# A decoder trunk on one core: every engine's order from a recorded plan instead of hand-set delays and a scheduler

## The chip, the cores and the metric

The kernel runs on one core of a Trainium2 chip. A core has four compute engines with a queue each: TensorE (PE in the profile; PEld is its loading of stationary operands), VectorE (DVE), ScalarE (ACT) and GpSimd (POOL). SyncE (SP) issues most DMAs, and ACT and POOL issue some. The metric is the time of one execution in device microseconds (us), lower is better. Before the change three runs took 1003.58, 1005.42 and 1005.6 us, a median of 1005.42 us.

## The reference, cut to what matters

A trunk of two layers over 256 tokens of width 1024, all in float32. Each layer is a SwiGLU FFN at half weight, a token mixer beside four memory cross-attention heads with one output projection, and a second FFN. Layer 0 mixes with an mLSTM (four heads), layer 1 with windowed attention (sixteen query heads, two key heads, a learned sink per head).

```
mem_kv = rms_norm(mem, mem_norm_g) @ mem_w_kv
for i in range(2):
    x = x + 0.5 * swiglu(rms_norm(x, ffn1_norm_g[i]), ffn1_w_in[i], ffn1_w_out[i])
    hn = rms_norm(x, mix_norm_g[i])
    proj = hn @ (a_w_in if i == 0 else b_w_in)
    y_tok = mlstm_heads(proj...) if i == 0 else swa_heads(proj...)
    y_mem = memory_heads(proj[..., -512:], mem_k, mem_v, ...)
    x = x + concatenate([y_tok, y_mem]) @ w_out
    x = x + 0.5 * swiglu(rms_norm(x, ffn2_norm_g[i]), ffn2_w_in[i], ffn2_w_out[i])
```

## The kernel before, in words

**Products.** Activations are held transposed, 128 features by 256 tokens a tile. Each float32 product with a weight is made of three products of rounded operands (`mm3`, L226): the high half of one side and of the other, and the two cross terms. So every weight tile of 128 x 1024 that a DMA brings (`wr`, five buffers, issued by SP at L220) is split: ACT casts it to its rounded half `wh` (L213) and DVE subtracts to get the rest, `wl` (L214). `wh` and `wl` have eight buffers each. A tile feeds 24 matmuls. In most stages the weight is the stationary operand; in the memory projection and in some groups of both mixers (`rows=True`) the activation is stationary and the weight moves.

**Stages.** `memory()` warms TensorE with 18 matmuls (L432), projects the memory and spawns the chains that finish its keys and the first norm. Then come FFN 1, mixer A, FFN 2, FFN 1 of layer 1, mixer B and the last FFN. In an FFN, `ffn_in` runs eleven groups of two PSUM banks, and `hidden` (L513) turns each into a unit. `out_proj` (L657) takes four banks at its first row of weights and waits, row by row, for the heads it multiplies.

**Chains.** Everything that isn't a weight product (norms, attention heads, transposes) is a Python generator, a chain, that yields an estimated delay in microseconds between its steps. `Weave` (L61) holds a clock `now`, which each matmul call advances by a fixed amount, and after every yield of the main program it runs the chain steps whose delay has passed. The delays are in `LAT` (L53). So the order of TensorE's queue is the order in which `Weave` calls things. In mixer B a head (L952) has three steps on TensorE: scores of two banks (L962, L967), six transposes (L995), and the product with the values (L1004).

**Who orders what.** `manual_schedule` (L1031) is given for PE and SP alone: these two issue in program order. DVE, ACT and POOL are ordered by the framework's scheduler, from its own model of durations. Three places bind it: a table load is issued after the last activation that needs the old table (L140), the copies of raw memory keys after the last weight cast (L455), the splits of x0 too (L490). All engines run their queues in order. PSUM has eight banks (`pb8`), one pool of 31 units (`up`) holds most intermediate tiles.

**Late constants.** `late_constants` (L184) is a chain called in the first FFN, at group 5. It has five small DMAs on POOL's queue and one of 192 KB (the mask), and small DVE operations on what they bring, among them `nsink` (L196).

Of the kernel before, what the change touches and what calls it, by code (L numbers as in the profile page):

```python
# [2 lines left out]

# [6 lines left out]

F32 = mybir.dt.float32
F32R = mybir.dt.float32r
# [48 lines left out]
class Weave:  # L61
# [4 lines left out]


    def __init__(self):
        self.now, self.live, self.seq = 0.0, [], 0

    def spawn(self, chain, delay=0.0):
        self.live.append([self.now + delay, self.seq, chain])
# [1 line left out]

    def step(self, c):
        self.now = max(self.now, c[0])
        try:
            c[0] = self.now + next(c[2])
        except StopIteration:
            self.live.remove(c)  # L80

    def ready(self):
        c = [c for c in self.live if c[0] <= self.now]
# [11 lines left out]
            self.step(min(self.live, key=lambda c: (c[0], c[1])))  # L95


@with_exitstack
def tile_trunk(ctx: ExitStack, tc: tile.TileContext, a, out):
    nc = tc.nc  # L100
    seq = [0]

    def mk(pool, shape, dt, tag):
        seq[0] += 1
        return pool.tile(shape, dt, tag=tag, name=f"{tag}_{seq[0]}")

    def pool(name, bufs, **kw):
        return ctx.enter_context(tc.tile_pool(name=name, bufs=bufs, **kw))

    cst = pool("cst", 1)  # L110
    onesr = mk(cst, [P, P], F32R, "onesr")
    nc.vector.memset(onesr.bitcast(F32), 1.0 / D)
    wv = Weave()


    xhp = pool("xhp", 4)
# [11 lines left out]
    pb8 = pool("pb8", 8, space=PSUM)  # L128

    tt = nc.vector.tensor_tensor  # L130
    tabled = [None]

    def act(*args, **kw):
        ins = nc.scalar.activation(*args, **kw)  # L134
        if args[2] not in (AF.Copy, AF.Square):
            tabled[0] = ins
# [66 lines left out]


    pieces = [1]
    last = [None]

    def split(src, shape):
        hi = mk(whp, shape, F32R, "wh")
        lo = mk(wlp, shape, F32R, "wl")  # L210
        n = shape[1] // pieces[0]
        for i in range(pieces[0]):
            last[0] = nc.scalar.copy(hi[:, i * n:(i + 1) * n], src[:, i * n:(i + 1) * n])  # L213
            tt(out=lo[:, i * n:(i + 1) * n], in0=src[:, i * n:(i + 1) * n],  # L214
               in1=hi[:, i * n:(i + 1) * n].bitcast(F32), op=ALU.subtract)
        return hi, lo
# [209 lines left out]
    def memory():  # L426

        idle = tmp().rearrange("p a b -> p (a b)")[:, :T].bitcast(BF16)
        nc.vector.memset(idle, 0.0)
        bank = mo()  # L430
        for i in range(WARM):
            nc.tensor.matmul(bank, idle[:, :P], idle, start=True, stop=True, skip_group_check=True)  # L432
# [72 lines left out]
        wv.spawn(sums(), LAT['x0'])  # L505
        wv.spawn(finish(raw), LAT['finish'])
# [513 lines left out]
    def program():  # L1020
        yield from memory()
        x1, x2, x3 = Norm(G_MIX, half=False, cols=True), Norm(G_F2), Norm(G_F1 + 8)
        x4, x5 = Norm(G_MIX + 8, rows=False), Norm(G_F2 + 8)
        yield from ffn(x0, a["ffn1_w_in"][0], a["ffn1_w_out"][0], x1, late_constants)
        yield from mixer_a(x1, x2)
        yield from ffn(x2, a["ffn2_w_in"][0], a["ffn2_w_out"][0], x3)
        yield from ffn(x3, a["ffn1_w_in"][1], a["ffn1_w_out"][1], x4, rope_tables)
        yield from mixer_b(x4, x5)
        yield from ffn(x5, a["ffn2_w_in"][1], a["ffn2_w_out"][1])

    with tc.manual_schedule(engines={mybir.EngineType.PE, mybir.EngineType.SP}):  # L1031
        wv.run(program())


def by_chunk(rows):
# [35 lines left out]
```

## Time and profile before

| | |
|---|---|
| median of three runs | 1005.42 us |
| the profiled execution, by its own time | 1004.76 us |
| its span, first to last instruction | 1003.0 us |
| granted TensorE clock | 1.00 |
| HBM read, over the span | 180.32 MB, 181 GB/s |
| PE instructions | 8560 matmuls, as many weight loads |
| DVE, ACT, POOL instructions | 1080, 779, 27 |

The span begins with the first instruction on any engine and leaves out 1.76 us of the execution's time. A line of the timeline has a start, a duration, engine, source line and tiles, and in brackets the idle time of that engine just before, with what ended it. Matmuls overlap: one of 256 columns is shown as 0.28 us long, while the next starts 0.11 us later, so starts are compared with starts. The line of an activation is often L134 and that of a weight product L227, L228 or L229, since a helper issues them; the tiles tell which is meant.

### The profile page before, as it was taken

What the parts mean: (1) busy time and instruction counts of PE and PEld (TensorE: products, weight loads), DVE (VectorE), ACT (ScalarE), POOL (GpSimd) and SP (SyncE); (2) the same over time, 40 slices, a digit from 0 to 9 for tenths busy, and PEclk for the clock granted to TensorE, in tenths of its full rate; (3) what the DMA queues carried; (4) which work ended last, traced back from release to release, by engine and by line L of the source; (5) the groups of instructions that cost most, each with busy time, mean ns of one, the idle gap of its engine ahead of it and who ended that gap; (6) DMA issues with size and microseconds to landing.
All of it is one profiled execution on the core that took longest, in us unless ns stands there. A gap on an engine that the chain in (4) does not pass through costs nothing.

```text
span 1003.0 us, 20581 instructions
## 1 busy us (share of the span) xinstructions
PE 993.9 (99%) x8560; PEld 975.7 (97%) x8560; DVE 664.6 (66%) x1080; ACT 531.9 (53%) x779; POOL 29.4 (3%) x27
## 2 busy tenths in 40 slices
PE   8999999999999999999999999999999999999998
PEld 6999999999999999999999999999997899999998
DVE  5897665578756686666568666656777767666551
ACT  5765445456666554444445444545577755544440
POOL 1001000000101000000000000000122000000000
PEclk9999999999999999999999999999999999999999
DMA  9777655666634566665666666566641247666550
GB/s 308 256 225 214 192 181 179 199 179 193 188 129 145 169 210 190 193 198 177 190 204 201 197 196 191 171 198 200 195 142 64 89 146 228 193 195 188 184 168 22
DMA packets 173204, 182.70 MB, mean 182 GB/s; under 512 B 7124, under 2 KB 168328, under 8 KB 173112
## 3 DMA queue, kind: packets, MB, share of 16 engines
q1 hardware_dynamic: 171872, 179.60, 57.8%
q8 instruction: 67, 1.10, 0.4%
q10 hardware_dynamic: 1016, 1.58, 0.4%
q0 software_dynamic: 224, 0.22, 0.2%
q14 instruction: 25, 0.20, 0.1%
HBM read 180.32 MB, written 1.05 MB: 181 GB/s over the span
## 4 chain that ended last, share of the span: by engine, by line
PE 93%; ACT 3%; DVE 2%; DMA 1%; issue 0%; SPq 0%; ACTq 0%; DVEq 0%
PE bank L227 30%; PE bank L229 30%; PE bank L228 30%; PE bank L233 2%; ACT u L134 1%; PE bank L238 1%; ACT wh L213 1%; DMA wr<-in_mem_w_kv_dram 1%; DVE wl L214 1%; PE bank L1004 1%; ACT xh L134 0%; DVE col L972 0%; DVE acc L282 0%; PE bank L304 0%; DVE col L971 0%
## 5 line engine op out<-in xcount | busy, mean ns | idle before, releaser
L214 DVE TENSOR_TENSOR wl<-wr,wh 128x1024 fp32r<-128x1024 f32 (+1 forms) x347 | 414.5, 1197 | 268.4 <-ACT wh L213 267.1
L213 ACT CAST wh<-wr 128x1024 fp32r<-128x1024 f32 (+1 forms) x347 | 356.9, 1031 | 385.8 <-PE bank L228 357.6
L227 PE MATMUL bank<-xh,wh 128*128 128x256 f32 x1544 | 428.0, 277 | 0.0
L229 PE MATMUL bank<-xh,wl 128*128 128x256 f32 x1544 | 426.8, 276 | 0.1
L228 PE MATMUL bank<-xl,wh 128*128 128x256 f32 x1544 | 426.7, 276 | 0.0
L229 PEld LDWEIGHTS bank<-xh,wl 128*128 128x128 f32 x1544 | 290.1, 188 | 0.3 <-DVE wl L214 0.3
L227 PEld LDWEIGHTS bank<-xh,wh 128*128 128x128 f32 x1544 | 290.0, 188 | 0.1
L228 PEld LDWEIGHTS bank<-xl,wh 128*128 128x128 f32 x1544 | 289.9, 188 | 0.1
L227 PE MATMUL bank<-u,wh 128*128 128x256 f32 x896 | 249.3, 278 | 0.0
L228 PE MATMUL bank<-u,wh 128*128 128x256 f32 x896 | 247.6, 276 | 0.0
L229 PE MATMUL bank<-u,wl 128*128 128x256 f32 x896 | 247.6, 276 | 0.0
L227 PEld LDWEIGHTS bank<-u,wh 128*128 128x128 f32 x896 | 168.3, 188 | 1.7 <-issue 1.7
L228 PEld LDWEIGHTS bank<-u,wh 128*128 128x128 f32 x896 | 168.3, 188 | 0.1
L229 PEld LDWEIGHTS bank<-u,wl 128*128 128x128 f32 x896 | 168.2, 188 | 0.0
L227 PE MATMUL bank<-wh,xh 128*128 128x256 f32 x208 | 59.6, 287 | 0.5 <-ACT t L997 0.5
L228 PE MATMUL bank<-wl,xh 128*128 128x256 f32 x208 | 57.9, 278 | 0.0
L229 PE MATMUL bank<-wh,xl 128*128 128x256 f32 x208 | 57.8, 278 | 0.0
L516 DVE TENSOR_TENSOR t<-bank,rb 128x256 f32<-128x256 f32 x88 | 36.1, 420 | 6.8 <-PE bank L229 6.8
L227 PEld LDWEIGHTS bank<-wh,xh 128*128 128x128 f32 x208 | 39.1, 188 | 1.2 <-ACT t L997 0.7
L228 PEld LDWEIGHTS bank<-wl,xh 128*128 128x128 f32 x208 | 39.1, 188 | 0.1
L229 PEld LDWEIGHTS bank<-wh,xl 128*128 128x128 f32 x208 | 39.0, 188 | 0.0
L134 ACT ACTIVATE u<-bank,col,col 128x256 f32<-128x256 f32 (+1 forms) x48 | 24.9, 530 | 15.2 <-DVE col L975 7.9
(183 smaller groups left out, 674.1 us busy)
## 6 DMA issues: line engine op xcount, KB each, us to landing
wr<-in_ffn_w_in_dram SPq DMA_DIRECT2D x176, 512.0 KB, 4.5
wr<-in_ffn_w_out_dram SPq DMA_DIRECT2D x80, 512.0 KB, 3.8
wr<-in_a_w_in_dram SPq DMA_DIRECT2D x28, 512.0 KB, 3.8
wr<-in_b_w_in_dram SPq DMA_DIRECT2D x14, 512.0 KB, 4.3
wr<-in_a_w_out_dram SPq DMA_DIRECT2D x12, 512.0 KB, 3.2
wr<-in_b_w_out_dram SPq DMA_DIRECT2D x12, 512.0 KB, 3.2
wr<-in_ffn_w_out_dram SPq DMA_DIRECT2D x16, 256.0 KB, 2.8
wr<-in_mem_w_kv_dram SPq DMA_DIRECT2D x7, 512.0 KB, 8.1
```

The source lines that it names most:

```text
L134: ins = nc.scalar.activation(*args, **kw)
L213: last[0] = nc.scalar.copy(hi[:, i * n:(i + 1) * n], src[:, i * n:(i + 1) * n])
L214: tt(out=lo[:, i * n:(i + 1) * n], in0=src[:, i * n:(i + 1) * n], in1=hi[:, i * n:(i + 1) * n].bitcast(F32), op=ALU.subtract)
L227: nc.tensor.matmul(ps, wh, xh, start=start, stop=False, skip_group_check=True)
L228: nc.tensor.matmul(ps, wh, xl, start=False, stop=False, skip_group_check=True)
L229: nc.tensor.matmul(ps, wl, xh, start=False, stop=stop, skip_group_check=True)
L233: nc.tensor.matmul(ps, lhsT, rhs, start=start, stop=stop, skip_group_check=True)
L238: nc.tensor.transpose(ps, src, ident[:k, :k])
L516: tt(out=t[:, m], in0=ps[m][:, :T], in1=x.rb, op=ALU.mult)
L1004: nc.tensor.matmul(o[es[e], cs], vr[:, i, js], pTs[e][:, src], start=i == 0, stop=i == 1, skip_group_check=True)
```

## The change

The program isn't issued while it is written. `tile_trunk` is run against a `Rehearsal`, whose engines only note each operation with the tiles that it reads and writes. `Weave` still gives the order in which operations are noted, and marks the chain step that each belongs to (`current`). From what each operation touches, `note` works out what it must follow. Then `plan` steps through all operations with a formula for each duration and returns one order, and `perform` issues the operations in it. `manual_schedule` now holds for all engines, so ACT, DVE and POOL too run in the planned order.

In `plan`, SP's DMAs keep their order. TensorE's work is cut into runs: an operation of the main program is a run of its own and these keep their order; a chain step is one run, and any of the first 24 not yet issued may go when its inputs are ready. A single chain run that is ready beside a ready main run is held back until a second one is ready, or for at most `HOLD` = 3 us. A main matmul that opens a new PSUM bank is passed over while `SPARE` = 2 or fewer banks are free and chain runs remain. On ACT, DVE and POOL the operation goes next that is ready and has the earliest `late` (the latest start that TensorE's order allows); none is planned more than `AHEAD` = 26 us before the matmul that follows it in the noted order. The three bindings of L140, L455 and L490 go; `note` keeps the order of table loads against the activations that need them. Tiles get their buffers in the order of issue. No instruction of the kernel is added or taken away.

```diff
@@ Weave.step
+        self.steps += 1
+        self.current = self.steps
         try:
             c[0] = self.now + next(c[2])
         ...
+        self.current = 0
@@ Rehearsal
+    def perform(self, order):
+        ...
+        for n in order:
+            op = self.ops[n]
+            getattr(getattr(nc, op.engine), op.kind)(*map(real, op.args), ...)
+    def note(self, engine, kind, args, kw):
+        ...
+        for write, vs in ((False, ins), (True, outs)):
+            for v in vs:
+                (a, b), (p0, p1) = v.extent(), v.parts
+                for o, c, d, q0, q1, w in v.tile.uses:
+                    same = o.engine == engine == "tensor"
+                    if (write or w) and (same or a <= d and c <= b and q0 < p1 and p0 < q1):
+                        behind(o, "data")
+        ...
+        if engine == "scalar":
+            if kind == "preload_act_table_set":
+                for o in self.tabled:
+                    behind(o, "order")
+                self.table, self.tabled = op, []
+            elif kind == "activation" and args[2] not in (AF.Copy, AF.Square):
+                if self.table is not None:
+                    behind(self.table, "order")
+                self.tabled.append(op)
@@ constants and durations
+AHEAD = 26.0
+SPARE = 2
+SWITCH = 0.1
+HOLD = 3.0
+OVERLAP = 0.085
+LATENCY = dict(tensor=0.25, vector=0.08, scalar=0.08, gpsimd=0.12, dma=0.0)
+def duration(op):
+    ...
+    if "dma" in kind:
+        return 0.06 if e != "gpsimd" else 0.6
+    if e == "tensor":
+        ...
+        if mv.dt == F32R:
+            return 0.1135 if st.tile.key[0] in ("wlp", "whp", "cst") else 0.117
+        if mv.dt == BF16 or st.dt == BF16:
+            return moving / 2400
+        half = st.shape[0] == 64 or st.shape[1] == 64
+        return moving * (0.00169 if not half else 0.00085)
+    if e == "vector":
+        ...
+        return 0.15 + 0.001045 * n + (0.09 if kind == "tensor_tensor_reduce" else 0)
+    if e == "scalar":
+        ...
+        t = 0.207 + 0.000825 * op.outs[0].size
+        ...
+    return 0.2 + 0.29 * n
@@ plan
+        if now:
+            found.append((free["tensor"], now[0], None))
+        else:
+            t0 = free["tensor"]
+            head = main[at["main"]] if at["main"] < len(main) else None
+            r0 = ready(head[0]) if head else None
+            if head and tiles_of[head[0].n] and side and len(places[tiles_of[head[0].n][0].key]) <= SPARE:
+                r0 = None
+            best, there = None, 0
+            for run in side[:24]:
+                r = run_ready(run)
+                if r is not None:
+                    there += r <= t0
+                    if best is None or max(r, t0) < best[0]:
+                        best = (max(r, t0), run, r)
+            if best and last_kind and there < 2 and t0 - best[2] < HOLD and r0 is not None and r0 <= t0:
+                best = None
+            if best and (r0 is None or best[0] <= max(r0, t0)):
+                found.append((best[0], best[1][0], best[1]))
+            elif r0 is not None:
+                found.append((max(r0, t0), head[0], head))
+        ...
+        for e in loose:
+            cand = []
+            for k, (n, op) in enumerate(loose[e].items()):
+                ...
+                r = ready(op)
+                if r is not None:
+                    cand.append((max(r, due[n] - AHEAD), op))
+            ...
+            t0 = max(free[e], min(c[0] for c in cand))
+            r, op = min((c for c in cand if c[0] <= t0), key=lambda c: (late[c[1].n], c[1].n))
+            ...
+            found.append((max(r, t0), op, None))
@@ tile_trunk and below
-        with tc.issue_after(tabled[0].ins):
-            nc.scalar.preload_act_table_set(name)
+        nc.scalar.preload_act_table_set(name)
-            with tc.issue_after(last[0].ins):
-                nc.scalar.copy(raw, gr.ps)
+            nc.scalar.copy(raw, gr.ps)
-                with tc.issue_after(last[0].ins):
-                    for c2 in range(4):
-                        x0.put(xT[c2], False)
+                for c2 in range(4):
+                    x0.put(xT[c2], False)
-    with tc.manual_schedule(engines={mybir.EngineType.PE, mybir.EngineType.SP}):
-        wv.run(program())
+    wv.run(program())
-    with tile.TileContext(nc) as tc:
-        tile_trunk(tc, aps, out)
+    with tile.TileContext(nc) as tc, ExitStack() as pools:
+        rec = Rehearsal(tc, aps["gd"])
+        tile_trunk(pools, rec, aps, out)
+        with tc.manual_schedule():
+            rec.perform(plan(rec))
```

More of the change, by code (lines that the diff above doesn't have):

```diff
@@ L1 @@
+import bisect
 import math
@@ L8 @@
 from concourse import mybir
-from concourse._compat import with_exitstack
 F32 = mybir.dt.float32
@@ L68, in __init__ @@
     def __init__(self):
-        self.now, self.live, self.seq = 0.0, [], 0
+        self.now, self.live, self.seq, self.current, self.steps = 0.0, [], 0, 0, 0
     def spawn(self, chain, delay=0.0):
@@ new lines, with __init__, real @@
+class Slot:
+    def __init__(self, pool, tag, number, shape, dt, name):
+        self.key, self.pool, self.number, self.uses, self.made = (pool.name, tag), pool, number, [], None
+        self.args = (shape, dt, tag, name)
+    def real(self):
+        if self.made is None:
+            shape, dt, tag, name = self.args
+            self.made = self.pool.real.tile(shape, dt, tag=tag, name=name)
+        return self.made
+class Op:
+    def __init__(self, engine, kind, outs, ins, args, kw):
+        self.engine, self.kind, self.outs, self.ins, self.args, self.kw = engine, kind, outs, ins, args, kw
+        self.after, self.before = {}, []
@@ new lines @@
+AHEAD = 26.0
[5 more added lines that the diff above has]
+def duration(op):
+    kind, e = op.kind, op.engine
+    n = max([v.size for v in op.outs + op.ins] or [0])
+    if "dma" in kind:
+        return 0.06 if e != "gpsimd" else 0.6
+    if e == "tensor":
+        moving = op.outs[0].size
+        if kind == "transpose":
+            return 0.109 if moving > 4 else 0.075
+        st, mv = op.args[1], op.args[2]
+        if mv.dt == F32R:
[5 more added lines that the diff above has]
+    if e == "vector":
+        if kind == "memset":
+            n = op.outs[0].size
+        if kind == "tensor_scalar" and op.ins[0].tile.key[1] != "bank" and n >= 128:
+            return 0.215 + 0.00052 * n
+        return 0.15 + 0.001045 * n + (0.09 if kind == "tensor_tensor_reduce" else 0)
+    if e == "scalar":
+        if kind == "preload_act_table_set":
+            return 1.283
+        t = 0.207 + 0.000825 * op.outs[0].size
+        views = sum(isinstance(op.kw.get(k), View) for k in ("scale", "bias"))
+        return t + 0.08 * views + (0.1 if "accum_out" in op.kw else 0)
+    return 0.2 + 0.29 * n
@@ L101, in tile_trunk @@
+def tile_trunk(ctx: ExitStack, nc, a, out):
     seq = [0]
@@ L107, in pool @@
     def pool(name, bufs, **kw):
-        return ctx.enter_context(tc.tile_pool(name=name, bufs=bufs, **kw))
+        return nc.pool(ctx, name, bufs, **kw)
     cst = pool("cst", 1)
+    wv = nc.weave = Weave()
     onesr = mk(cst, [P, P], F32R, "onesr")
     nc.vector.memset(onesr.bitcast(F32), 1.0 / D)
-    wv = Weave()
     xhp = pool("xhp", 4)
@@ L130, in tile_trunk @@
     tt = nc.vector.tensor_tensor
[L131 to L136, printed above, removed]
+    act = nc.scalar.activation
     def table(name):
-        with tc.issue_after(tabled[0].ins):
-            nc.scalar.preload_act_table_set(name)
+        nc.scalar.preload_act_table_set(name)
     def unit(dt):
@@ L205, in tile_trunk @@
     pieces = [1]
-    last = [None]
     def split(src, shape):
@@ L212, in split @@
         for i in range(pieces[0]):
-            last[0] = nc.scalar.copy(hi[:, i * n:(i + 1) * n], src[:, i * n:(i + 1) * n])
+            nc.scalar.copy(hi[:, i * n:(i + 1) * n], src[:, i * n:(i + 1) * n])
             tt(out=lo[:, i * n:(i + 1) * n], in0=src[:, i * n:(i + 1) * n],
```

278 lines of the change are left out of this document (275 added, 3 removed).

## The prediction

> **What bounds the kernel now.** The first page shows which engine fills the span.
>
> ```profile
> span 1003.0 us, 20581 instructions
> ...
> PE 993.9 (99%) x8560; PEld 975.7 (97%) x8560; DVE 664.6 (66%) x1080; ACT 531.9 (53%) x779; POOL 29.4 (3%) x27
> ...
> PE 93%; ACT 3%; DVE 2%; DMA 1%; issue 0%; SPq 0%; ACTq 0%; DVEq 0%
> ```
>
> TensorE is busy for 99% of the span and holds 93% of the chain that ended last. The change takes no instruction away, so it can only remove time in which TensorE stands still. Two views size that: what TensorE waited for, and its busy time by stage.
>
> ```profile
> engine line waited for: us in total, times, longest us
> PE bank L967 <- ACT u L134: 1.4, 1, 1.4
> PE bank L432 <- DVE t L429: 1.4, 1, 1.4
> PE bank L228 <- DVE wl L214: 0.9, 1, 0.9
> PE bank L227 <- ACT t L997: 0.5, 1, 0.5
> PE bank L227 <- ACT wh L213: 0.4, 1, 0.4
> PE bank L962 <- ACT t L997: 0.2, 1, 0.2
> ```
>
> Those are all of TensorE's waits over 0.15 us, 4.8 us together. The second is the wait for the first memset at the very start, which stays. The third and fifth belong to the first weight tiles. The other three, 2.1 us, are in mixer B.
>
> ```profile
> core 0: us, PE busy (x) PEld busy (x) DVE busy (x) ACT busy (x) POOL busy (x), PEclk, DMA share, GB/s
> 330.00:715.00 385.00, 385.00 (x3399) 385.00 (x3398) 252.28 (x333) 192.21 (x234) 0.00 (x0) 1.00 0.63 193
> 735.00:765.00 30.00, 27.99 (x209) 23.86 (x208) 23.93 (x80) 24.57 (x74) 3.84 (x2) 1.00 0.22 76
> 765.00:795.00 30.00, 29.64 (x249) 24.44 (x248) 21.17 (x74) 21.08 (x59) 5.08 (x2) 1.00 0.32 102
> ```
>
> From 330 to 715 us there is nothing to win: 385.00 of 385.00 us are busy, 0.113 us a matmul, at clock 1.00. In mixer B TensorE idles 30.00 - 27.99 + 30.00 - 29.64 = 2.37 us. So the whole reach of a better order is mixer B's 2.4 us and the start.
>
> **Part 1: the host side.** Recording, `View`, `Slot` and `plan` run before the launch and cost the chip nothing. The numbers of instructions stay.
>
> **Part 2: the start, and DMAs that move.** The start is this chain.
>
> ```profile
> 1.37 6.54 PE L432 MATMUL bank<-t 128*128 128x512 bf16 x18 [1.37 <-DVE t L429]
> ...
> 7.61 0.17 DVE L196 TENSOR_SCALAR nsink<-sink 128x16 f32<-128x16 f32 x1 [4.70 <-DMA sink<-in_b_sinks_dram]
> ...
> 8.27 1.82 ACT L134 ACTIVATE u<-u,gcol 128x256 fp32r<-128x256 f32 x4 [0.53 <-DMA u<-in_memT_dram]
> ...
> 11.03 1.05 ACT L213 CAST wh<-wr 128x1024 fp32r<-128x1024 f32 x1 [0.95 <-DMA wr<-in_mem_w_kv_dram]
> ...
> 12.11 1.23 DVE L214 TENSOR_TENSOR wl<-wr,wh 128x1024 fp32r<-128x1024 f32 x1 [0.73 <-ACT wh L213]
> ...
> 13.39 0.39 PE L228 MATMUL bank<-wl,u 128*128 128x256 f32 x1 [0.88 <-DVE wl L214]
> ```
>
> TensorE runs steadily from 13.39 us, when the first full weight tile has landed (11.03), been cast (1.05) and subtracted (1.23). ACT waited for DMAs twice before it. DVE stood 4.70 us before `nsink`, an operation needed only in mixer B, put at the head of its queue while its DMA was under way. The plan gives `nsink` a `late` hundreds of microseconds on, so this block goes; but the first matmuls wait for the warming anyway (1.37 to 7.9), so alone it brings nothing.
>
> What can bring something is the DMAs behind it. In the order noted, POOL's five small DMAs come after the reciprocal root of the memory norm (L309), since `late_constants` is spawned in the first FFN. The scheduler drew them to 1.4 us. The plan holds them until 26 us before their next matmul, by my reckoning of the noted order near 70 us, by when the memory norm should be ready, so they queue behind L309 on POOL. What they cost now stands in the DMA queues of two stretches, 4 to 9 us and 9 to 14 us.
>
> ```profile
> q1 hardware_dynamic: 951, 1.17, 66.5%
> q0 software_dynamic: 125, 0.02, 32.1%
> ```
>
> ```profile
> q1 hardware_dynamic: 1773, 1.92, 107.1%
> ```
>
> In the first stretch POOL's queue took 32.1% of the engines' time for 0.02 MB, while SP's moved 1.17 MB; in the second SP's alone moved 1.92 MB. If all of the 32.1% went to SP's queue, its transfers would land 0.321 x 5 = 1.6 us earlier. If the slow stretch is only the queue filling, they gain nothing. I take -1.0 us, nearer the full value, because the queue was saturated (98.6% together) and the weight tile was issued early. The cast can follow: ACT would end its splits about 0.5 us sooner, at 9.6, and the tile would land at 10.0. **Start: -1.0 (-1.6 to 0).** The moved DMAs run beside the first FFN and go nowhere near an urgent transfer.
>
> **Part 3: chain steps when ready.** Mixer B's longest stall:
>
> ```profile
> 755.17 0.93 PE L967 MATMUL bank<-u,u 64*128 64x128 f32 x8 [1.45 <-ACT u L134]
> 756.03 0.38 PE L227 MATMUL bank<-wh,xh 128*128 128x256 f32 x1
> ```
>
> A head's scores stand at the front of the queue 1.45 us before their queries are ready, while weight products of a query group follow at 756.03. `LAT` guessed too early. A plan that issues a step when its inputs are there puts those products first. The two shorter waits in the list above, 0.5 and 0.2 us, are of the same kind: a step's copy not done. ACT itself is late there, since it stood for DVE's maxima:
>
> ```profile
> ACT u L134 <- DVE col L975: 7.9, 5, 3.0
> ```
>
> Ordering DVE by need shortens these 7.9 us, and what is late next is ACT, busy 24.57 of 30 us. I take 1.8 of the 2.4 us. **Mixer B: -1.8 (-2.4 to 0).**
>
> **Part 4: holding single steps.** The plan charges 0.1 us when TensorE changes between rounded and plain operands, and holds a lone step for up to 3 us to share that. The trace shows no such cost:
>
> ```profile
> 732.54 0.28 PE L229 MATMUL bank<-wh,xl 128*128 128x256 f32 x1
> 732.66 1.03 PE L233 MATMUL bank<-kT,u 128*128 128x256 f32 x4
> 733.33 0.47 PE L227 MATMUL bank<-wh,xh 128*128 128x256 f32 x1
> 733.64 0.28 PE L228 MATMUL bank<-wl,xh 128*128 128x256 f32 x1
> ```
>
> ```profile
> 259.92 0.86 PE bank L233 x4
> ```
>
> From 732.54 to 733.64 are 1.10 us. Four plain matmuls take 0.86 on the chain and two weight products 0.12 each: 1.10. So sharing gains 0, and the delay is hidden by weight products, which must be ready for the hold to apply. Without that cover a held step would cost up to 3 us. **0.**
>
> **Part 5: durations the plan relies on.** Most agree with rows above: a cast of 1024 columns is planned at 0.207 + 0.845 = 1.052 us and took 1.05, a subtraction at 1.22 and took 1.23. POOL's power doesn't:
>
> ```profile
> L402 POOL TENSOR_TENSOR col<-col,mhalf 128x4 f32<-128x4 f32 x7 | 11.1, 1583 | 176.5 <-DVE col L400 176.5
> ```
>
> The plan has 0.2 + 0.29 x 4 = 1.36 us, 0.22 less than the mean, so DVE can stand that long with a power's consumer at its head and weight subtractions behind. Seven times that is 1.6 us; eight buffers of `wl` hide most. **New waits: +0.2 (0 to 1.6).** The Trainium skill, in SBUF — State Buffer, Who interferes with whom, says that GpSimd and a VectorE operation with two SBUF inputs lock each other out of a shared port, which would make any fixed POOL duration wrong beside subtractions; by that reading the term would go towards its upper end. The spread behind the mean fits, though no row here shows the lock itself.
>
> The three removed bindings put copies and splits where `late` puts them; the table loads keep their order by `note`. I cost these at 0: they lie beside weight products at both places. Were the cover gone, a copy would cost the 1.05 us of a cast.
>
> **Sum.** -1.0 - 1.8 + 0.2 = -2.6 us against the profiled execution's 1004.76 us: **1002.2 us**. Its span was 1003.0, with 1.76 us around it, which stay. The median before is 1005.42, so the forecast is 0.32% under it. With both gains in full and no new wait it would be 1004.76 - 4.0 = 1000.8.
>
> **Rivals.**
> *The waits only move.* ACT and DVE are busy 24.57 and 23.93 of 30 us in the worst stretch and each head's steps wait for one another, so a filled hole reopens at the next head; and the start is the queue filling. For it: mixer B's largest wait ends on a chain of DVE and ACT. Against it: weight products stood right behind. 1004.76 - 0.3 = 1004.5.
>
> *Banks held back: slower.* A main matmul opens a bank only with three or more free. `out_proj` opens four at its first row, so at the fourth it goes only if other steps hold two at most, the score banks of one head. Heads started as early as possible hold more. Then TensorE lacks its only filler until a head lets go, from its scores at 755.17 to the last exponential:
>
> ```profile
> 759.84 0.20 ACT L134 ACTIVATE col<-col 128x4 f32<-128x4 f32 x1
> ```
>
> That is 4.9 us for one missed opening; it decides once heads hold three banks when the fourth opens. With the start's gain and none in mixer B: 1004.76 - 1.0 + 4.9 = 1008.7. Against it: of TensorE's waits in the list none over 0.5 us falls to a weight product, the kind that opens these banks, after the start.
>
> *More room than the busy time shows.* Loading stationary operands was idle in mixer B for 30 - 23.86 + 30 - 24.44 = 11.70 us; if that were all standstill, the time would be 1004.76 - 11.70 = 993.1. Against it: plain matmuls start 0.215 us apart (0.86 for four) and fill it. The Trainium skill, in Perfetto Trace Analysis, Identifying the Most-Contended Engine, judges TensorE's headroom by this share and not by matmul busy time. The rows above disagree with that for this stretch.
>
> **How the numbers follow.** Forecast 0.48, waits only move 0.32, banks 0.17, more room 0.03. About 0.2% (2 us) is what a measurement can tell from no change: faster means under 1003.4, slower over 1007.4. The forecast and "more room" are faster: 0.51. "Waits only move" is within: 0.32. Banks are slower: 0.17. As these are on both sides, the forecast's own range is 1000.8 to 1003.4. The full range goes from 999.0, 1.8 us under its best sum for rows read too short, to 1008.7, the banks' price.
>
> **What would show it.** Right at the start: no DVE wait before `nsink`, POOL's DMAs after L309, the first steady matmul near 12.4 us instead of 13.39. In mixer B: no wait of TensorE over 0.5 us, and a busy time above 29.5 of 30 us. Banks: a gap of several microseconds before the first row of `out_proj`. I am wrong if the steady start doesn't move, if ACT or DVE stand at the head for something the plan thought ready, or if stalls appear in the FFNs, where there were none.

## The result, and the profile after

The kernel after takes 1020.20 us (median of 4 runs, 1019.83 to 1022.51), the one before 1005.51 us beside it: 1.0155 times as long, 95% interval 1.0136 to 1.0175. The forecast was 1002.2 us with a range of 999.0 to 1008.7. The profiled execution took 1020.51 us with a span of 1018.7.

The page of the kernel after, with the share of the span of each engine and the chain that ended last. Every line is L234 now, since one function issues all operations; the tiles tell the groups apart.

```profile
span 1018.7 us, 20684 instructions
...
PE 1007.0 (99%) x8560; PEld 985.3 (97%) x8560; DVE 668.0 (66%) x1080; ACT 532.3 (52%) x779; POOL 27.5 (3%) x27
...
PE 97%; DVE 1%; DMA 1%; ACT 1%; issue 0%; SPq 0%; ACTq 0%; DVEq 0%
```

TensorE is as busy as before, 99%, and holds more of the chain, 97% against 93%. The same 8560 matmuls fill 1007.0 us instead of 993.9. So most of the 15.7 us aren't idle time in this view. What TensorE waited for, in the kernel after:

```profile
engine line waited for: us in total, times, longest us
PE bank L234 <- DVE t L234: 3.0, 5, 1.2
PE bank L234 <- ACT v L234: 2.4, 4, 0.6
PE bank L234 <- DVE u L234: 1.0, 2, 0.5
PE bank L234 <- DVE wl L234: 0.9, 1, 0.9
PE bank L234 <- ACT wh L234: 0.4, 1, 0.4
PE bank L234 <- ACT u L234: 0.2, 1, 0.2
```

The first three rows are new but for one wait at the start. They are short, though, 7.9 us for the whole list against 4.8 before. The place of the rest shows when the busy time is cut into windows inside the FFNs and matmuls are counted. Before, then after:

```profile
400.00:500.00 100.00, 100.00 (x885) 1.00 0.61 189
600.00:700.00 100.00, 100.00 (x885) 1.00 0.62 190
880.00:980.00 100.00, 100.00 (x885) 1.00 0.58 180
```

```profile
400.00:500.00 100.00, 100.00 (x871) 1.00 0.61 187
600.00:700.00 100.00, 100.00 (x873) 1.00 0.61 186
880.00:980.00 100.00, 100.00 (x871) 1.00 0.61 187
```

Busy 100.00 of 100.00 us at clock 1.00 in both, yet the kernel after starts 871 to 873 matmuls where the one before starts 885. A full busy column says only that a matmul was always open; the count in brackets says how fast they went.

The table cuts the traces of both kernels, and of three experiments told below, at the first weight product of each stage (these products keep their order and number, 8136). It runs from the start of the span to the start of the last product. "FFN 2 and 1" is the second FFN of layer 0 with the first of layer 1.

| stage, us | before | after | e1 | e10 | e9 |
|---|---|---|---|---|---|
| start, to FFN 1 | 33.30 | 31.90 | 32.10 | 31.99 | 31.68 |
| FFN 1 | 182.04 | 184.54 | 181.95 | 183.32 | 181.32 |
| mixer A | 133.05 | 139.58 | 134.80 | 138.61 | 133.87 |
| FFN 2 and 1 | 359.49 | 366.82 | 373.23 | 370.73 | 359.49 |
| mixer B | 111.33 | 107.88 | 108.57 | 107.91 | 108.25 |
| last FFN | 179.63 | 183.84 | 186.32 | 182.58 | 179.63 |

Start and mixer B gained 1.4 and 3.5 us. The FFNs lost 2.5 + 7.3 + 4.2 = 14.0 us and mixer A 6.5. The starts of the matmuls in "FFN 2 and 1" show two kinds of loss. Before, every weight product there starts 113.3 ns after the last, but for two places where a norm chain enters. After, 34 more intervals are longer than 120 ns, 4.4 us too long in sum; and 655 lie between 116 and 120 ns in long stretches, 2.9 us too long. 4.4 + 2.9 = 7.3. Over the whole kernel, 945 intervals are of the second kind before and 2607 after.

**The long intervals** look so in the timeline of the kernel after, at one of the FFN's groups (start, duration, engine; weight loads, PEld, beside the matmuls):

```profile
387.26 0.42 DVE L234 TENSOR_TENSOR t<-bank,rb 128x256 f32<-128x256 f32 x1
...
387.66 0.28 PE L234 MATMUL bank<-xh,wl 128*128 128x256 f32 x1
387.80 0.19 PEld L234 LDWEIGHTS bank<-xh,wh 128*128 128x128 f32 x1
387.83 0.36 PE L234 MATMUL bank<-xh,wh 128*128 128x256 f32 x1
...
387.98 0.43 DVE L234 TENSOR_TENSOR t<-bank,rb 128x256 f32<-128x256 f32 x1 [0.30 <-PE bank L234]
388.02 0.28 PE L234 MATMUL bank<-xl,wh 128*128 128x256 f32 x1
```

DVE multiplies the gate half of a group's bank by `rb` (L516 of the kernel before). The next weight load starts at 387.80, after DVE's end at 387.68; the matmuls start 0.17 and 0.19 us apart instead of 0.113. The up half of that bank is still to be computed. `note` tracks dependences by bytes, so the plan thinks that TensorE may write one half while DVE reads the other; the program as built has a wait there, because the bank is one tile. In mixer A, ACT does the same with half a bank of `v`:

```profile
294.48 0.28 PE L234 MATMUL bank<-wh,xl 128*128 128x256 f32 x1
294.80 0.47 ACT L234 ACTIVATE v<-bank,rc 128x256 f32<-128x256 f32 x1 [0.67 <-PE bank L234]
...
295.32 0.39 PE L234 MATMUL bank<-wh,xh 128*128 128x256 f32 x1 [0.56 <-ACT v L234]
```

TensorE stands from its last product to ACT's end at 295.27. Before the change both reads came after the whole bank was written, in the noted order. **The second kind**, a pace of 117.8 ns that lasts for hundreds of matmuls, had no cause in sight. The experiments take the two apart.

### The profile page after: what moved, and what is told of

Its sections match the earlier page's. It is cut to its first block, busy times and chain, and to the rows that moved or that the text cites. A ratio compares the mean times of both kernels' runs of the same rounds, so it can differ in the third digit from the quotient of the medians.

```text
span 1018.7 us, 20684 instructions
## 1 busy us (share of the span) xinstructions
PE 1007.0 (99%) x8560; PEld 985.3 (97%) x8560; DVE 668.0 (66%) x1080; ACT 532.3 (52%) x779; POOL 27.5 (3%) x27
## 3 DMA queue, kind: packets, MB, share of 16 engines
q10 hardware_dynamic: 1016, 1.58, 0.5%
## 4 chain that ended last, share of the span: by engine, by line
PE 97%; DVE 1%; DMA 1%; ACT 1%; issue 0%; SPq 0%; ACTq 0%; DVEq 0%
PE bank L234 97%; DMA wr<-in_mem_w_kv_dram 1%; DVE u L234 0%; ACT wh L234 0%; SPq L234 0%; DVE t L234 0%; DVE wl L234 0%; ACT v L234 0%; ACT u L234 0%; ACTq L234 0%; DVEq L234 0%
## 5 line engine op out<-in xcount | busy, mean ns | idle before, releaser
L234 DVE TENSOR_TENSOR wl<-wr,wh 128x1024 fp32r<-128x1024 f32 (+1 forms) x349 | 414.7, 1190 | 251.2 <-ACT wh L234 249.0
L234 ACT CAST wh<-wr 128x1024 fp32r<-128x1024 f32 (+1 forms) x349 | 357.2, 1025 | 406.0 <-PE bank L234 382.9
L234 PE MATMUL bank<-xh,wh 128*128 128x256 f32 x1544 | 431.9, 280 | 0.8 <-DVE u L234 0.5
L234 PE MATMUL bank<-xl,wh 128*128 128x256 f32 x1544 | 429.9, 278 | 2.1 <-DVE t L234 1.5
L234 PE MATMUL bank<-xh,wl 128*128 128x256 f32 x1544 | 429.4, 278 | 0.0
L234 PE MATMUL bank<-u,wh 128*128 128x256 f32 x1792 | 308.0, 277 | 0.0
L234 PEld LDWEIGHTS bank<-xh,wh 128*128 128x128 f32 x1544 | 290.4, 188 | 4.4 <-issue 2.5
L234 PEld LDWEIGHTS bank<-xl,wh 128*128 128x128 f32 x1544 | 290.5, 188 | 2.9 <-DVE t L234 2.2
L234 PEld LDWEIGHTS bank<-xh,wl 128*128 128x128 f32 x1544 | 291.1, 189 | 0.0
L234 PEld LDWEIGHTS bank<-u,wh 128*128 128x128 f32 x1792 | 270.3, 188 | 1.2 <-issue 1.2
L234 PE MATMUL bank<-u,wl 128*128 128x256 f32 x896 | 248.0, 277 | 0.0
L234 PEld LDWEIGHTS bank<-u,wl 128*128 128x128 f32 x896 | 168.2, 188 | 0.0
L234 PE MATMUL bank<-wh,xh 128*128 128x256 f32 x208 | 59.1, 284 | 1.8 <-ACT v L234 1.8
L234 PE MATMUL bank<-wl,xh 128*128 128x256 f32 x208 | 58.4, 281 | 0.6 <-ACT v L234 0.6
L234 PE MATMUL bank<-wh,xl 128*128 128x256 f32 x208 | 58.8, 283 | 0.0
L234 DVE TENSOR_TENSOR t<-bank,rb 128x256 f32<-128x256 f32 x88 | 36.2, 420 | 20.9 <-PE bank L234 20.4
L234 DVE TENSOR_TENSOR t<-t,bank 128x256 f32<-128x256 f32 x88 | 36.1, 417 | 16.9 <-PE bank L234 13.0
L234 PEld LDWEIGHTS bank<-wh,xh 128*128 128x128 f32 x208 | 39.1, 188 | 2.5 <-ACT v L234 2.4
L234 DVE TENSOR_TENSOR u<-t,u 128x512 fp32r<-128x512 f32 (+1 forms) x59 | 40.2, 684 | 0.3
L234 PEld LDWEIGHTS bank<-wl,xh 128*128 128x128 f32 x208 | 39.0, 188 | 0.9 <-ACT v L234 0.8
L234 PEld LDWEIGHTS bank<-wh,xl 128*128 128x128 f32 x208 | 39.1, 188 | 0.5 <-issue 0.5
L234 POOL TENSOR_TENSOR col<-col,mhalf 128x4 f32<-128x4 f32 (+2 forms) x15 | 21.3, 1425 | 299.5 <-DVE col L234 299.5
```

Of the source, the lines that this page charges most:

```text
L234: getattr(getattr(nc, op.engine), op.kind)(*map(real, op.args), **{k: real(x) for k, x in op.kw.items()})
```

## The experiments

Each ran beside the kernel before on one chip; ratios are to it, with a 95% interval. Slow intervals are those of 116 to 120 ns between the starts of one weight product and the next, counted in the trace. The expectations use a slightly wider count, 991 before and 6026 in e1 for what is 945 and 5984 here.

**e1: whole banks.** The plan is told what the built program does.

```diff
-                    same = o.engine == engine == "tensor"
-                    if (write or w) and (same or a <= d and c <= b and q0 < p1 and p0 < q1):
+                    same, bank = o.engine == engine == "tensor", v.tile.key[1] == "bank"
+                    if (write or w) and (same or bank or a <= d and c <= b and q0 < p1 and p0 < q1):
```

> The changed kernel with one edit: in the record of dependences, two operations on the same PSUM tile of which one writes it now conflict whatever parts of the bank they touch. Theory A (the plan lets DVE and ACT read one half of a bank while TensorE has still to write the other half; on the chip the whole bank is one object, so TensorE waits for the reader in every FFN group and in mixer A): TensorE's waits on DVE t, DVE u and ACT v (3.0, 1.0 and 2.4 us in the changed kernel) vanish, the FFNs run again without a break, and the time falls from 1020.2 to 998-1004 us. Theory B (DVE's and ACT's queues are ordered by lateness with durations that are a little off, so banks come free too late whatever is recorded): the breaks at the starts of FFN groups stay and the time stays above 1014 us. Theory C (buffers are handed out in another order than the plan thinks): as B.

1022.47 us, ratio 1.018 (1.0164 to 1.0195). TensorE's waits in e1:

```profile
PE bank L234 <- DVE t L234: 1.2, 1, 1.2
PE bank L234 <- DVE wl L234: 0.9, 1, 0.9
PE bank L234 <- ACT wh L234: 0.3, 1, 0.3
```

The waits for half-read banks are gone, as expected, and no interval in "FFN 2 and 1" is over 120 ns but for the two that hold a norm chain. The expected 998 to 1004 us didn't come, since the pace is worse: 5984 slow intervals.

```profile
100.00:200.00 100.00, 100.00 (x885) 1.00 0.61 190
400.00:500.00 100.00, 100.00 (x852) 1.00 0.57 182
600.00:700.00 100.00, 100.00 (x851) 1.00 0.57 180
880.00:980.00 100.00, 100.00 (x852) 1.00 0.57 184
```

A stretch runs at 885 or at 852, with nothing between. So what was taken for one loss is two, and in the kernel after the stalls of the first kind had ended some of the second: after a stall the pace may be either. In its trace the pace turns from slow to fast at a group's stall at 399 us and from fast to slow at another at 454 us.

**e2: the half-bank read planted into the kernel before.**

```diff
                         yield
+                    if kh == 1 and part == 0 and x.done:
+                        t = tmp()
+                        for m in range(2):
+                            tt(out=t[:, m], in0=ps[m][:, :T], in1=x.rb, op=ALU.mult)
+                        early[id(ps)] = t
```

> The kernel before, with hand-set delays and the scheduler, and one edit: in the FFNs' input groups the two multiplications of the gate half by the row factor (L516) are issued when the gate half is complete, ahead of the last 24 matmuls, which write the up half of the same two banks. Theory A: this alone brings the breaks into the kernel before, 0.25 to 0.55 us in most of some 40 groups, with a slower pace of matmuls behind each: 1012 to 1025 us. Theories B and C: DVE's order hardly differs, so 1003.5 to 1007.5 us.

1022.85 us, ratio 1.0187 (1.0172 to 1.0202). The waits gain this row, against none on `t` of the FFNs over 0.15 us before:

```profile
PE bank L227 <- DVE t L544: 7.5, 4, 5.7
```

The groups' intervals lengthen as in the kernel after (38 over 120 ns in "FFN 2 and 1", 5.5 us). The planted read, without plan or holding, costs this kernel 18 us. Half of that falls in the first FFN, which is 9.2 us longer and shows more than the groups' price: 5.7 us are one wait, from 52.9 to 58.6 us, until DVE has the row factor `rb`. The kernel after doesn't have this wait, and behind it the granted clock is 0.50 from 58 to 62 us. "FFN 2 and 1" and the last FFN, 6.1 and 2.9 us longer, show the groups' stalls by themselves. The slower pace that was expected behind each stall hardly came, 1050 slow intervals against 945.

**e3: no holding.** e1 with `HOLD = 0.0` and `SWITCH = 0.0`.

> As e1_whole_bank, with HOLD and SWITCH at 0: a chain step goes as soon as it is ready, and the plan charges nothing for changing between rounded and plain operands. If changing costs nothing, as rows of the kernel before say, the time is within 1.5 us of e1_whole_bank. If it does cost about 0.1 us a change, it is 2 to 4 us slower.

1010.06 us, ratio 1.0057 (1.0042 to 1.0072), 2715 slow intervals: 885 matmuls per 100 us in the middle FFNs, 852 in the last. Dropping the hold moved the pace, which pointed at how a chain step enters TensorE's queue.

**e4: POOL's DMAs first**, e1 with these planned as soon as they can go.

```diff
-                    cand.append((max(r, due[n] - AHEAD), op))
+                    cand.append((r if e == "gpsimd" and "dma" in op.kind else max(r, due[n] - AHEAD), op))
```

> As e1_whole_bank, with POOL's small DMAs of the late constants planned as soon as they can go, so that they run at about 1.4 us as in the kernel before. If they hold up SP's first transfers, the first steady matmul comes 0.8 to 1.6 us later than in e1_whole_bank and the time is 0.8 to 1.6 us longer. If the slow stretch is only the queue filling, both are within 0.4 us.

1020.47 us, ratio 1.0158 (1.0141 to 1.0175). FFN 1 begins at 37.88 us instead of e1's 32.10, with this wait:

```profile
PE bank L234 <- ACT wh L234: 4.0, 1, 4.0
```

So holding POOL's DMAs back is worth 5.8 us at the start of this plan, far more than the expected 0.8 to 1.6, and the total hides it in a better pace elsewhere (4347 slow intervals). It isn't the price of the kernel before, though. e4 runs six DMAs there, the mask of 192 KB first, at 1.25 us; the kernel before ran the five small ones, and the mask at 84.4 us. And after the wait the granted clock is 0.50 from 14 to 20 us, where e1 has 1.00.

**e5, e6, e7: where a chain step enters.** In e1 the pace always turned at the two matmuls of a norm chain (`bank<-u,onesr`, L304 before), which the plan had put into the middle of an accumulation of 12. e5 lets them enter only where the main program yields:

```diff
-            if not op.step or not runs or runs[-1][0].step != op.step:
+            if not runs or runs[-1][0].step != op.step or not op.step and runs[-1][0].seg != op.seg:
```

> e1 (whole-bank dependences) with the main program's TensorE work planned in pieces that are never cut: a chain step can enter only where the main program yields, after a full accumulation of 12 matmuls, as in the kernel before. Theory D (a chain step, above all the norm chain's two rounded matmuls, put into the middle of an accumulation turns TensorE from the pace of 113.3 ns to that of 117.8 ns, and it stays there): intervals of 116 ns or more fall from e1's 6026 to below 1500, and with 22 us of them gone the time is 998 to 1004 us. Rival T (the pace falls by chance of the spacing at any side step, wherever it enters): more than 2500 slow intervals stay, 1008 to 1022 us. Rival H (the held steps, HOLD and SWITCH, start it, as their absence made e3 faster): as T, and only e7 is fast.

e6 does the opposite to the kernel before, by three more yields in each group of 12:

```diff
                                 start=kc == 0 and part == 0, stop=kc == 7)
+                            if k < 3:
+                                yield
                         yield
```

> The kernel before with three more yields in each group of 12 matmuls of the FFNs' first half, so that its chain steps can enter between any two sets of three; the amount of work is the same, nothing is planned. Theory D: the norm chain's two matmuls fall inside an accumulation in most FFNs, the pace drops to 117.8 ns after them, and each FFN so hit loses up to 1584 x 4.4 ns = 7 us: 1010 to 1033 us, slow intervals above 2500 (991 before). Rivals T and H: nothing is held and the steps come at about the same times, so 1003 to 1007 us, slow intervals near 1000.

e7 is e5 without holding.

> e5 with HOLD and SWITCH at zero, so that single steps aren't held. Theory D: the same pace as e5, 998 to 1004 us. Rival H: 998 to 1004 us where e5 is at 1008 to 1022. Rival T: about e3's 1010.

e5 took 1021.00 us (1.0162; 1.0147 to 1.0178) with 5960 slow intervals, e6 1004.73 (1.0006; 0.9996 to 1.0016) with 782, e7 1022.93 (1.0183; 1.0166 to 1.02) with 5784. Theory D fell twice: at yields the pace turns all the same, and in the middle of accumulations it doesn't. Nor is it the hold. At the norm chain near 357 us the order of matmuls is alike in e5 and before, and TensorE waits in neither; what was left was the data's place. The Python class `Slot` makes a tile at its first issue, and so the constants, which lie one behind the other in one pool, had changed places with the issue order. `onesr`, the stationary operand of those two matmuls, had moved. The built programs give these first bytes in SBUF, here modulo 128:

```
kernel     onesr   wh, wl   xh, xl, u
before       0       0         64
after       64       0         64        (onesr at 18368; before at 16512)
e4          96       0         64
e8          64       0         64
e9, e10      0       0         64
e11          0       0          0
e14         64      64          0
e16          0       0         64
```

**e8: one tile moved in the kernel before.**

```diff
-    onesr = mk(cst, [P, P], F32R, "onesr")
+    onesr = mk(cst, [P, P + 32], F32R, "onesr")[:, 16:16 + P]
```

> The kernel before with one edit: the tile onesr, the stationary operand of the norm chains, starts 64 bytes further on in its row of SBUF (16576 = 64 mod 128 instead of 16512 = 0 mod 128), and the tiles behind it move by 128 bytes. Order, instructions and waits are those of before. Theory L (a weight load from an address that is no multiple of 128 bytes comes late and turns TensorE from the pace of 113.3 ns to that of 117.8 ns; in the kernel after, onesr lies at 18368 = 64 mod 128, since tiles are made in the order of their first issue): the pace drops at each of the six norm chains that it survived before, the slow intervals rise from 991 to 4500 or more, the time to 1019 to 1028 us. Rival O (order, holding or waits of the planned program set the pace): 1003.5 to 1006 us, slow intervals near 1000.

1019.69 us, ratio 1.0159 (1.0144 to 1.0174), 4167 slow intervals. Order and instructions are those of before; TensorE's waits add up to 5.3 us against 4.8. The norm chain at 358 us, in e8 and below it in the kernel before:

```profile
358.47 0.28 PE L228 MATMUL bank<-xl,wh 128*128 128x256 f32 x1
358.59 0.28 PE L229 MATMUL bank<-xh,wl 128*128 128x256 f32 x1
358.70 0.39 PE L304 MATMUL bank<-u,onesr 128*128 128x256 f32 x2
358.94 0.28 PE L227 MATMUL bank<-xh,wh 128*128 128x256 f32 x1
359.05 0.28 PE L228 MATMUL bank<-xl,wh 128*128 128x256 f32 x1
359.17 0.28 PE L229 MATMUL bank<-xh,wl 128*128 128x256 f32 x1
359.29 0.28 PE L227 MATMUL bank<-xh,wh 128*128 128x256 f32 x1
```

```profile
357.91 0.39 PE L304 MATMUL bank<-u,onesr 128*128 128x256 f32 x2
358.14 0.28 PE L227 MATMUL bank<-xh,wh 128*128 128x256 f32 x1
358.25 0.28 PE L228 MATMUL bank<-xl,wh 128*128 128x256 f32 x1
358.36 0.28 PE L229 MATMUL bank<-xh,wl 128*128 128x256 f32 x1
358.48 0.28 PE L227 MATMUL bank<-xh,wh 128*128 128x256 f32 x1
```

The starts are read against each other. Before: 357.91 to 358.48 are five steps from start to start (the first row stands for two matmuls), 0.57 / 5 = 0.114. In e8 358.70 to 359.29 are five too, 0.59 / 5 = 0.118, and it stays so to the next chain. A shift of 64 bytes, with no instruction changed, costs 15.8 us.

**e9, e10: the constants where they lay before**, made in the program's order ahead of the first instruction; e9 on e1, e10 on the kernel after.

```diff
+        for slots in self.slots.values():
+            if slots[0].key[0] == "cst":
+                slots[0].real()
         for n in order:
```

> e1 (whole-bank dependences) with the constants' tiles made in the program's order before the first instruction is issued, so that they lie where they lay in the kernel before (onesr at 16512); the plan is that of e1. Theory L: slow intervals fall from 6026 to about 1000 to 1600, 20 us of e1's 1022.5 go: 998 to 1004 us, no drop of the pace at a norm chain. Rival O: 1018 to 1024 us.

> The kernel after with the constants' tiles where they lay before, nothing else: the half-bank reads stay. Theory L with the half-bank stalls as the other part of the loss: of 15.7 us the 1659 slow intervals more than before (7.3 us at 4.4 ns) go and the breaks and waits at half-read banks stay: 1009 to 1016 us. If the half-bank reads cost nothing by themselves: 1000 to 1004 us. Rival O: 1019 to 1022 us.

e9: **999.86 us, ratio 0.9956 (0.9939 to 0.9973)**, 951 slow intervals. e10: 1019.46 us (runs from 1016.34 to 1025.13), ratio 1.0159 (1.0123 to 1.0195), 2601. With the kernel after and e1 this is a square:

| | constants as issued | constants as before |
|---|---|---|
| half banks | 1020.20 (after) | 1019.46 (e10) |
| whole banks | 1022.47 (e1) | 999.86 (e9) |

Neither cure shortens the time alone, both together take 20 us. In e10 the groups' stalls themselves throw the pace, to slow in the stretch from 400 to 500 us:

```profile
400.00:500.00 100.00, 100.00 (x847) 1.00 0.57 182
```

and in e1 the chains throw it with nothing to bring it back. My expectation for e10, 1009 to 1016, treated the two as terms of a sum. In e9 the FFNs of the table are those of before to 0.01 us, or better:

```profile
400.00:500.00 100.00, 100.00 (x885) 1.00 0.59 189
```

**e11: all stationary operands at multiples of 128.** Two tiles made larger move what lies behind them.

```diff
-    warm = mk(cst, [P, 1], F32, "warm")
+    warm = mk(cst, [P, 24], F32, "warm")[:, :1]
-            v = mk(vp, [P, 2, T + 2], F32, "v")
+            v = mk(vp, [P, 2, T + 6], F32, "v")
```

> e9 with two tiles made a little larger, so that every stationary operand of a rounded matmul (u, xh, xl, kT, the bf16 identity) starts at a multiple of 128 bytes too, where in before they start at 64 mod 128. Theory L: the slow intervals that before has as well (991, 4.4 us, in the memory stage and in the mixers' row forms) go too: 994 to 1000 us, slow intervals below 500. Rival M (only onesr matters): as e9 within 1 us.

1039.24 us, ratio 1.0353 (1.0338 to 1.0369), the worst of all, by the opposite of what I expected. No stretch is fast; all four windows of 100 us read 845:

```profile
600.00:700.00 100.00, 100.00 (x845) 1.00 0.56 179
```

So, it seems, not the address counts but its difference to that of the operand that streams past while the weights load. In e11 every weight load has the stream's own place modulo 128; with `onesr` at 64 in the kernel after, two loads for each norm chain have.

**e14, e16, e15: the last word on place, and on the hold.** e14 moves all tiles of the kernel before by 64 bytes together (`[P, P + 16]`, `[:, 16:]` at `onesr`). e16 is e1 with e8's edit, by which `onesr` alone leaves the place 64.

> The kernel before with onesr and every tile behind it moved by 64 bytes together: onesr and wh, wl go from 0 to 64 mod 128, xh, xl and u from 64 to 0 mod 128; order and instructions are those of before. Theory R (the weight load is disturbed by the moving operand that is streamed at the same time, where the two addresses are equal mod 128; the difference counts): all differences are as before, so 1003 to 1006 us, no drop of the pace at the norm chains, slow intervals near 1000. Rival A (the stationary operand's own address must be a multiple of 128): every weight tile is off, 1019 us or more.

> e1 (whole-bank dependences; constants in the order of first issue) with onesr alone moved 64 bytes on, from 18368 (64 mod 128, as xh, xl and u) to 18432 (0 mod 128, as wh and wl); the tiles behind it move by 128 bytes, all other differences mod 128 stay. Theory R: the norm chains no longer turn the pace, 998 to 1003 us, slow intervals 900 to 1700. Rival C (another of the constants that e9 moved is the cause): 1015 to 1023 us.

e14: 1005.52 us (1.0004; 0.9994 to 1.0014), 806 slow intervals, though every weight tile lies at 64. e16: 1001.28 us (0.9966; 0.9955 to 0.9978), 955. A difference decides, and `onesr` alone accounts for 21 of e1's 22.6 us above e9. The difference to the stationary operand loaded just before would explain e8, e14, e16 and e4 as well. Against it stands e11 alone, where the stationary operands of weight products and norm chains all lie at 0 and no stretch is fast. e15 is e9 without holding.

> e9 (whole-bank dependences, constants where they lay before) with HOLD and SWITCH at zero. If holding costs nothing once the pace is kept, as the prediction's part 4 said: within 1.5 us of e9's 999.9. If holding itself costs, as e3 against e1 seemed to show: 996 us or less. If holding saves TensorE's changes between rounded and plain matmuls: 1001.5 or more.

1009.96 us (1.0066; 1.0039 to 1.0093), where the last expectation put it, but not for its reason: 7.1 of the 9.5 us that its profile has above e9's are the last FFN, run at the slow pace, which was entered in mixer B and never left. Two of its six runs took 1016 us, some 6 us more, which no profile shows.

```profile
600.00:700.00 100.00, 100.00 (x885) 1.00 0.61 190
880.00:980.00 100.00, 100.00 (x851) 1.00 0.56 180
```

## Why the prediction was wrong, by its own steps

**What bounds.** Right that no instruction goes and TensorE bounds. The sentence "From 330 to 715 us there is nothing to win" was true and read too narrowly: nothing to win, but in FFN 2 and 1, most of that stretch, 7.3 us to lose. I took 0.113 us a matmul for given, and it was a property of this layout and this order.

**Part 1, the host side, 0.** This is the step that failed first. Recording costs the chip nothing, but `Slot` also decides in which order tiles are made, and with it their addresses. I listed `Slot` and passed on. Its price in e8, on the kernel before, is 15.8 us.

**Part 2, the start, -1.0.** Right in sign, and undersized. The steady start moved from 13.39 to 12.13 us (12.4 forecast), DVE no longer stands before `nsink`, and to FFN 1 the gain is 1.4 us, 1.6 in e9. The timeline of the kernel after has the start and POOL's DMAs where I expected them, behind the root and near 70 us:

```profile
12.13 0.39 PE L234 MATMUL bank<-wl,u 128*128 128x256 f32 x1 [0.87 <-DVE wl L234]
```

```profile
70.08 0.72 POOL L234 DMA_DIRECT2D u<-in_mask_dram  x1
```

e4 shows that these DMAs can hold up the start, by 5.8 us with the mask among them and half the clock behind the wait. How much of the 1.4 us comes from the five small ones, and how much from ACT and DVE going in another order, no run tells.

**Part 3, mixer B, -1.8.** Right, and the size was low: 3.5 us in the kernel after and 3.1 in e9. None of the waits in the list above lies there, and the stretch that idled is full:

```profile
750.00:780.00 30.00, 30.00 (x240) 26.32 (x239) 21.76 (x69) 21.84 (x55) 5.16 (x3) 1.00 0.32 106
```

The idle time of 2.37 us that I called the whole reach was too small a bound, since intervals inside "busy" shrank too. The rival "the waits only move" is out, and so is "banks held back": no gap at `out_proj`. That one had the right side and the wrong place.

**Part 4, the hold, 0.** No direct cost could be separated. With and without it the time differs by 12.4 us one way (e3 below e1) and 10.1 the other (e15 above e9), each time mostly by the pace in which FFNs ran.

**Part 5, new waits, +0.2 (0 to 1.6).** The term that was mis-sized. I checked the plan's durations against rows and not its dependences. POOL's power made no wait; the reads of half banks did: in the kernel after they stretch intervals by about 1.1 us in FFN 1, 4.4 in FFN 2 and 1, 4.5 in mixer A and 2.1 in the last FFN (intervals over 120 ns with no chain step between, less those before), 12.2 us together. In the same stages the slow pace adds 7.2 us (4.4 ns for each slow interval more), and the intervals that hold chain steps 1.2. 12.2 + 7.2 + 1.2 = 20.6, less the 4.9 us gained: the 15.7 us by which the profile grew. The text named the sign itself, "if stalls appear in the FFNs, where there were none", and gave it no chance of its own.

With both defects cured the gains that were forecast come through: e9's 999.86 us lies under the 1002.2, and just under the forecast's own range from 1000.8, by the larger gains at the start and in mixer B.

## What to carry to other kernels

Where a planner replaces a scheduler, compare its dependences with those that the framework enforces before its durations: a finer rule than the enforced one orders work into waits. Whatever changes the order in which tiles are made moves addresses; keep the layout fixed when the order is what is tried. In a stretch that is 100% busy, count instructions per microsecond, since busy time doesn't show a pace.

## What the hardware showed that was not expected

TensorE has three paces for the same rounded matmuls of 256 columns, each with its weight load, at a granted clock of 1.00: 113.3 ns between starts (before, 400 to 530 us), 117.8 (e1, same stretch) and 118.7 (e11). The first two hold by themselves: after a disturbance of some 5 ns at one weight load, the pace stayed slow for up to some 1600 matmuls (e8, from 358.6 to 545 us). The disturbance came where the stationary operand's first byte equals the streamed operand's modulo 128 (e8, e11), not where both moved together (e14). e4, 32 bytes apart, was disturbed as well, 64 apart was not. That isn't the whole rule: in the kernel before, where mixer A's products change from stationary weights to streamed ones, one weight load has the stream's place too. At 240.0 us the next intervals are 114 and 115 ns and the pace stays fast; at 250.9 us, at the change back, one is 119 ns and the pace turns slow. The Trainium skill, in TensorE: Matmul & The Clock Gate, Step-by-step: what each phase is for, gives TensorE two independent read ports, one for the stream and one for the weights. e11 against e9, 118.7 against 113.3 ns with only places changed, shows that their timing depends on the two places together; that it is the ports where they meet, no run shows.

The Trainium skill, in PSUM — Partial Sum Buffer, PSUM bank collisions raise a hardware error, has it that access by two engines must be guarded by bank, not by address. The waits of the kernel after, which go in e1, agree with a program built by that rule.

Open: why a pace lasts, what brings the fast one back (in e9 it returned in mixer B near 804 us, in e8 at a norm chain at 545 us, and in e15 not at all behind 790 us), and whether the modulus is 128 or the part of it that the distances 0, 32 and 64 can tell. The 951 slow intervals that e9 still has, 4.2 us in all, in the memory stage, the beginning of FFN 1 and the mixers, weren't pursued.
